# The mixers' row scales: column sums by a ones matrix, or one-column products and transposes

## The chip, the cores and the metric

The kernel runs on one core of one Trainium2 chip. The metric is the device time of one execution in microseconds (us). The engines are named as the profile names them: PE is TensorE (its matmuls), PEld its loads of the stationary operand, DVE is VectorE, ACT is ScalarE, POOL is GpSimd, and SP is SyncE, whose queue issues the loads of the weights.

## What is computed

A decoder trunk of two layers over 256 tokens and 1024 channels in float32. Each layer is a half-step FFN, a mixer and a second half-step FFN:

```python
for l in range(DEPTH):
    x = x + 0.5 * swiglu_ffn(x, ffn1_norm[l], ffn1_wi[l], ffn1_wo[l])
    h = rms_norm(x, mix_norm[l])
    (sb_q, sb_k, sb_v, mla_cq, ..., merge_gate) = jnp.split(h @ w_in[l], offsets, axis=-1)
    o_sb, o_mla, o_nsa = ...                  # three attentions on parts of h @ w_in
    y = sum of sigmoid(gate_i) * (o_i @ proj_i)
    x = x + y @ w_out[l]
    x = x + 0.5 * swiglu_ffn(x, ffn2_norm[l], ffn2_wi[l], ffn2_wo[l])
```

What matters here is the norm at the head of the mixer. `rms_norm(x, g)` divides each token's row by the root of its mean square over the 1024 channels and multiplies by the gain `g`. The division is by one number per token, so the kernel leaves it out of the projection and applies it to the projection's results.

## The kernel before

`x` is kept transposed: channels on the 128 partitions, in eight blocks, with the 256 tokens (two tiles of 128) along the row. Products are taken in `fp32r` from a high and a low half of each operand (`mm3` and its like: high by high, high by low, low by high). ACT makes the high half by a copy, DVE the low half by a subtraction. Weights come from HBM as parts of 128 by at most 512 (`raw`, six buffers, issued by SP) and are split by ACT (`whi`, line 998 in a mixer) and DVE (`wlo`, line 1000).

**How the squares come about.** At the end of an FFN, `out_T` adds the output to `x` (line 675), makes the halves `hThi` and `hTlo` of `x` times the gain for what follows (lines 599 and 600), and gathers the squares in the tile `sq`: ACT squares (line 608), DVE adds (lines 610 and 612), so that `sq[:, 0:256]` holds for each token 128 partial sums, one on each partition.

**The scales.** `scales` (line 1063) makes of it what the mixer needs, once per mixer. It splits `sq` into two halves (`split`, lines 573 and 574), and `col_sums` (line 614) multiplies a matrix of ones by both halves, which puts every token's sum of squares on all 128 partitions (tile `att`). `row_scales` (line 623) picks the diagonal with the identity (line 626), reduces it to a sum per token with tokens on the partitions (line 628), scales it (line 630), takes the power -1/2 on POOL (line 632), and makes three multiples of the result, `rn` (line 635). It then puts `rn` on the diagonal again (line 636) and splits that into the same two halves. A second `col_sums` spreads it over all partitions with the tokens along the row (tile `tp`), and ACT copies it to `rows` (tile `rowm`, line 1084). `rn` scales results that have tokens on the partitions, `rows` those that have them along the row.

**What sets the order.** In a mixer the order of PE, ACT and DVE is laid down while the kernel is built, by a small planner (`Planner`): each piece of work is a generator that asks, by `yield`, for an engine with a length, a latency, the events it depends on, and buffers. The planner grants the request that can start first by its own clock, adjusted by a hold for each generator (`HOLDS`), and the generator then issues its instructions. Each engine runs them in that order. The instructions that a generator issues behind one request stand together, also those on another engine than the one it asked for. `scales` comes first among the generators. Its first request is only for a `wr` buffer, and the split of `sq` follows at once; `col_sums` comes at the request of line 1070, all of `row_scales` at that of line 1073, and the second `col_sums` at that of line 1080 (`use_t(2, ...)`), with a request for POOL (line 1076) and two for DVE (lines 1077 and 1079) between, behind which nothing is issued.

**What runs around it.** `bulk` issues the projections: `lat` (line 1119) with 440 columns in `mm3` (lines 578 to 580), which uses the first four slabs of weights, two of them converted already in the FFN, and then `chunk_T` with 256 columns (lines 1159 to 1161). `weights` issues the loads and conversions of the slabs. `ev_lat` (line 1088) takes up the results of `lat` with `rn`, `sb_qk` (line 1167) those of `chunk_T` with `rows`.

The FFNs have a chain of their own with the same helpers (`spread_rn`, `scale_cols`).

Of the kernel before, what the change touches and what calls it, by code (L numbers as in the profile page):

```python
# [10 lines left out]
F = mybir.dt.float32  # L11
R = mybir.dt.float32r
AF = mybir.ActivationFunctionType
OP = mybir.AluOpType
AX = mybir.AxisListType

D = 1024
S = 256
DEPTH = 2
DFF = 2816  # L20
EPS = 1e-6
NT = 2
# [285 lines left out]
def use_v(n, *deps, slots=()):  # L308

    return "V", 0.065 + 0.00106 * n, 0.15 + 0.00106 * n, deps, slots  # L310
# [7 lines left out]
def use_a(n, *deps, slots=()):  # L318

    return "A", 0.085 + 0.00085 * n, 0.19 + 0.00085 * n, deps, slots  # L320
# [13 lines left out]
def use_t(count, *deps, slots=()):  # L334

    o = 0.2 + count * 0.109
    return "P", o, o + 0.2, deps, slots


def use_g(us, *deps, slots=()):  # L340

    return "G", us, us, deps, slots
# [13 lines left out]
MOVING = 48  # L356
# [5 lines left out]
NG = 3 * DEPTH * KT  # L362
# [9 lines left out]
def decoder_trunk(ctx, tc, xt_in, wts, lcon, cst, out, depth=DEPTH):  # L372
    nc = tc.nc
# [4 lines left out]
    sm = ctx.enter_context(tc.tile_pool(name="sm", bufs=5))  # L378
# [9 lines left out]
    def tp_tile():  # L388
        return pb.tile([128, 512], F, tag="ps", name="tp")

    def att_tile():
        return pb.tile([128, 512], F, tag="ps", name="att")
# [15 lines left out]
    ident = cp.tile([128, 128], F, name="ident")  # L408
# [33 lines left out]
    mh = cp.tile([128, 16], F, name="mh")  # L442
    nc.vector.memset(mh, -0.5)
    gcol = cp.tile([128, 128], F, name="gcol")
    ones = cp.tile([128, 128], R, name="ones")
    nc.vector.memset(ones.bitcast(F), 1.0)

# [124 lines left out]
    def split(hi, lo, src):  # L572
        nc.scalar.activation(hi, src, AF.Copy)
        nc.vector.tensor_sub(lo, src, hi)
# [39 lines left out]
    def col_sums(q, o):  # L614

        for i in range(2):
            nc.tensor.matmul(o, ones, q[i], start=i == 0, stop=i == 1)

    def ident2():

        return ident[:, None, :].to_broadcast([128, NT, 128])

    def row_scales(a, sq, parts):

        d = sq[:, 0:S].rearrange("p (t n) -> p t n", t=NT)
        nc.vector.tensor_tensor(d, a[:, 0:S].rearrange("p (t n) -> p t n", t=NT), ident2(), op=OP.mult)
        cs = sm.tile([128, 16], F, tag="mn", name="cs")
        nc.vector.tensor_reduce(cs[:, 0:NT], d, axis=AX.X, op=OP.add)
        ss = sm.tile([128, 16], F, tag="ss", name="ss")
        nc.vector.tensor_scalar(ss[:, 0:NT], cs[:, 0:NT], 1.0 / D, EPS, op0=OP.mult, op1=OP.add)  # L630
        r = sm.tile([128, 16], F, tag="rs", name="rs")
        nc.gpsimd.tensor_tensor(r[:, 0:NT], ss[:, 0:NT], mh[:, 0:NT], op=OP.pow)
        q = hp.tile([128, 8], F, tag="rn", name="rn", bufs=4)
        for i, m in enumerate((1.0, 0.5, 0.125)):
            nc.vector.tensor_scalar(q[:, 2 * i:2 * i + 2], r[:, 0:2], m, None, op0=OP.mult)
        nc.vector.tensor_tensor(d, ident2(), q[:, 0:2, None].to_broadcast([128, NT, 128]), op=OP.mult)
        split(*parts, sq[:, 0:S])
        return [q[:, 0:6].rearrange("p (m t) -> p m t", t=NT)[:, :, t] for t in range(NT)]

    nxt = [None]  # L640
# [63 lines left out]
    def ffn(l, gi):  # L704
# [5 lines left out]
        with ExitStack() as es:  # L710
# [71 lines left out]
            def scale_cols():  # L782
                a = att_tile()
                col_sums(sqr, a[:, 0:S])
                rn[:] = row_scales(a, sq, sqr)
# [118 lines left out]
    def mixer(l):  # L904
        es = ExitStack()
        mp = es.enter_context(tc.tile_pool(name="mp", bufs=1))
        hT, sq = nxt[0]
        nxt_T = hT
        hT = of_t(hT)
        rn = [None] * NT  # L910
        xd = dp.tile([NT, 128, D], F, tag="xd", name="xd")

        def wf():
            return mp.tile([128, 384], F, tag="wf", name="wf", bufs=4)

        def wr():
            return mp.tile([128, 2, 384], R, tag="wr", name="wr", bufs=WR_BUFS)
# [34 lines left out]
        s_wf, s_wr, s_qk, s_th, s_tmp, s_of = Slots(4), Slots(WR_BUFS), Slots(4), Slots(TH_BUFS), Slots(1), Slots(1)  # L952
# [109 lines left out]

        def scales():

            yield "-", 0.0, 0.0, (), (s_wr,)
            w = wr()
            sqr = [w[:, i, MOVING:MOVING + S] for i in range(2)]
            split(*sqr, sq[:, 0:S])
            k = yield "P", 0.4, 0.6, (Tok(10.5), ev_used[3]), (s_tp,)
            a = att_tile()  # L1070
            col_sums(sqr, a[:, 0:S])
            k = yield "V", 0.1, 0.17, (k,), ()
            rn[:] = row_scales(a, sq, sqr)
            s_tp.put(k)
            k = yield use_g(1.5, k)
            k = yield "V", 0.3, 0.4, (k,), ()
            ev_rn.set(k)
            k = yield use_v(256, k)
            k = yield use_t(2, k, slots=(s_tp,))
            tp = tp_tile()  # L1080
            col_sums(sqr, tp[:, 0:S])
            s_wr.put(k)
            k = yield use_a(256, k)
            nc.scalar.activation(rows, tp[:, 0:S], AF.Copy)
            s_tp.put(k)
            ev_rows.set(k)
# [931 lines left out]
        for th, hold in zip((scales(), tables(), sb_T(), sb_scores(), sb_pv(), cmp_in(), nsa_prep(), gates(), mla_T(),  # L2018
                             mla_scores(), mla_P(), mla_pv(), nsa_T(), k_chain(), v_chain(), cmp_scores(), nsa_scores(),
                             nsa_P(), nsa_pv(), bulk()), HOLDS):  # L2020
            spawn(th, hold)
# [57 lines left out]
```

## Time and profile before

| | |
|---|---|
| median of three timed runs | 1270.21 us (1269.59 to 1271.56) |
| the profiled execution, its own time | 1272.12 us |
| its span, from the first to the last instruction | 1270.2 us |
| PE busy | 1252.7 us, 99% |
| DVE, ACT busy | 940.2 us (74%), 787.8 us (62%) |
| HBM read, written | 254.91 MB, 34.60 MB |

A line of the timeline has the start in us from the beginning of the span, the length in us, the engine, the line of the kernel, the operation, what it writes and reads, the shape, and the number of like instructions that follow one another (their length is then that of the whole row); in brackets stands for how long the engine had been idle and what ended that. A matmul's start on PE follows its load on PEld, and neighbours overlap, so that 256 columns last 0.28 us each but follow one another at 0.11 us.

### The profile page before, as it was taken

The page shows a single profiled execution, that of the slowest core. Times are in us where ns is not written, and L with a number is a line of the kernel's source. Part 1 is how long each engine was busy: PE and PEld are TensorE (multiplying, and loading weights), DVE is VectorE, ACT ScalarE, POOL GpSimd, SP SyncE. Part 2 cuts the span into 40 slices and gives each one's busy share as a digit, 9 for nine tenths or more (in the row PEclk, how much of TensorE's full clock was granted, in tenths as well). Part 3 has the DMA queues.
Part 4 walks back from the last instruction along what each step waited for, and adds up shares of the span by engine and source line. Part 5 has one row for each costly group of instructions (what it writes and reads, how often), then busy time and mean ns, then how long its engine had stood idle before and what let it go on. Part 6 is the DMA issues. An engine that isn't in the chain of part 4 may idle for free.

```text
span 1270.2 us, 26119 instructions
## 1 busy us (share of the span) xinstructions
PE 1252.7 (99%) x9373; PEld 1167.5 (92%) x9373; DVE 940.2 (74%) x1963; ACT 787.8 (62%) x1632; POOL 105.5 (8%) x164
## 2 busy tenths in 40 slices
PE   9999998999999999999999999999999999999998
PEld 9999998888877899999999999988888779999987
DVE  7866677988898777676678676779868886776643
ACT  6555555687877566555556565567757774565542
POOL 0011110210000001122000121011100000000000
PEclk9999999999999999999999999999999999999999
DMA  8779985647545568899857899565786455666753
GB/s 285 261 273 331 323 298 175 199 151 238 188 125 172 173 206 257 278 325 334 282 201 267 290 327 346 190 206 168 251 289 216 142 174 181 186 186 194 217 163 119
DMA packets 150961, 291.76 MB, mean 230 GB/s; under 512 B 17840, under 2 KB 19504, under 8 KB 150832
## 3 DMA queue, kind: packets, MB, share of 16 engines
q1 hardware_dynamic: 140976, 258.12, 63.0%
q0 software_dynamic: 9856, 31.99, 6.5%
q8 instruction: 73, 1.20, 0.4%
q14 instruction: 56, 0.46, 0.1%
HBM read 254.91 MB, written 34.60 MB: 228 GB/s over the span
## 4 chain that ended last, share of the span: by engine, by line
PE 89%; DVE 4%; ACT 4%; DMA 2%; issue 1%; POOL 0%; ACTq 0%; DVEq 0%; POOLq 0%
PE acc L747 12%; PE acc L746 12%; PE acc L745 12%; PE acc L578 8%; PE acc L580 8%; PE acc L579 8%; PE acc L658 6%; PE acc L656 6%; PE acc L657 6%; DMA raw<-in_wts 1%; PE tp L1605 1%; PE acc L1159 1%; PE acc L1160 1%; PE acc L1161 1%; ACT wf L1564 1%
## 5 line engine op out<-in xcount | busy, mean ns | idle before, releaser
L745 PE MATMUL acc<-hThi,vhi 128*128 128x256 f32 x1280 | 354.1, 277 | 0.0
L746 PE MATMUL acc<-hTlo,vhi 128*128 128x256 f32 x1280 | 353.5, 276 | 0.0
L747 PE MATMUL acc<-hThi,vlo 128*128 128x256 f32 x1280 | 353.5, 276 | 0.0
L526 DVE TENSOR_TENSOR vlo<-raw,vhi 128x512 fp32r<-128x512 f32 x452 | 292.1, 684 | 74.7 <-ACT vhi L525 71.4
L525 ACT ACTIVATE vhi<-raw 128x512 fp32r<-128x512 f32 x452 | 263.0, 622 | 123.9 <-DMA raw<-in_wts 35.8
L745 PEld LDWEIGHTS acc<-hThi,vhi 128*128 128x128 f32 x1280 | 240.4, 188 | 0.0
L746 PEld LDWEIGHTS acc<-hTlo,vhi 128*128 128x128 f32 x1280 | 240.3, 188 | 0.0
L747 PEld LDWEIGHTS acc<-hThi,vlo 128*128 128x128 f32 x1280 | 240.2, 188 | 0.0
L1000 DVE TENSOR_TENSOR wlo<-raw,whi 128x512 fp32r<-128x512 f32 x216 | 140.3, 678 | 27.5 <-ACT whi L998 26.2
L998 ACT ACTIVATE whi<-raw 128x512 fp32r<-128x512 f32 x216 | 124.9, 616 | 44.0 <-issue 16.5
L658 PE MATMUL acc<-gh,vlo 128*128 128x256 f32 x528 | 146.4, 277 | 0.4 <-DVE vlo L526 0.3
L656 PE MATMUL acc<-gh,vhi 128*128 128x256 f32 x528 | 146.3, 277 | 0.0
L657 PE MATMUL acc<-gl,vhi 128*128 128x256 f32 x528 | 146.2, 277 | 0.0
L578 PE MATMUL acc<-whi,hThi 128*128 128x512 f32 (+2 forms) x352 | 137.7, 391 | 3.1 <-ACT whi L998 3.1
L579 PE MATMUL acc<-wlo,hThi 128*128 128x512 f32 (+2 forms) x352 | 133.6, 380 | 0.5 <-DVE wlo L1000 0.5
L580 PE MATMUL acc<-whi,hTlo 128*128 128x512 f32 (+2 forms) x352 | 133.6, 379 | 0.0
L545 DVE TENSOR_TENSOR elo<-eraw,ehi 128x512 fp32r<-128x512 f32 x60 | 41.4, 689 | 97.6 <-ACT ehi L544 97.6
L544 ACT ACTIVATE ehi<-eraw 128x512 fp32r<-128x512 f32 x60 | 37.9, 631 | 117.5 <-DMA eraw<-in_wts 116.1
L526 DVE TENSOR_TENSOR wlo<-raw,whi 128x512 fp32r<-128x512 f32 x108 | 69.9, 682 | 43.2 <-ACT whi L525 42.6
L658 PEld LDWEIGHTS acc<-gh,vlo 128*128 128x128 f32 x528 | 99.1, 188 | 0.8 <-DVE vlo L526 0.8
L657 PEld LDWEIGHTS acc<-gl,vhi 128*128 128x128 f32 x528 | 99.5, 188 | 0.0
L656 PEld LDWEIGHTS acc<-gh,vhi 128*128 128x128 f32 x528 | 99.1, 188 | 0.2 <-ACT vhi L525 0.2
(342 smaller groups left out, 2483.5 us busy)
## 6 DMA issues: line engine op xcount, KB each, us to landing
raw<-in_wts SPq DMA_DIRECT2D x764, 256.0 KB, 3.5
eraw<-in_wts SPq DMA_DIRECT2D x60, 256.0 KB, 5.3
early<-ehi POOLq DMA_DIRECT2D x60, 256.0 KB, 3.7
early<-elo POOLq DMA_DIRECT2D x60, 256.0 KB, 4.3
whi<-early SPq DMA_DIRECT2D x60, 256.0 KB, 3.9
wlo<-early SPq DMA_DIRECT2D x60, 256.0 KB, 4.0
xd<-x SPq DMA_DIRECT2D x4, 512.0 KB, 2.6
x<-xd SPq DMA_DIRECT2D x4, 512.0 KB, 3.7
```

The costliest lines, as they stand in the source:

```text
L525: nc.scalar.activation(hi[:, c:c + m], raw[:, :m], AF.Copy)
L526: nc.vector.tensor_tensor(lo[:, c:c + m], raw[:, :m], hi[:, c:c + m], op=OP.subtract)
L578: nc.tensor.matmul(o, a[0], b[0], start=start, stop=False)
L579: nc.tensor.matmul(o, a[0], b[1], start=False, stop=False)
L580: nc.tensor.matmul(o, a[1], b[0], start=False, stop=stop)
L656: nc.tensor.matmul(o, sl[0][:, w], h, start=k == 0 and c == 0, stop=False)
L657: nc.tensor.matmul(o, sl[0][:, w], l_, start=False, stop=False)
L658: nc.tensor.matmul(o, sl[1][:, w], h, start=False, stop=k == kts - 1 and c == 1)
L745: nc.tensor.matmul(o, sl[0][:, w], h, start=k == 0 and c == 0, stop=False)
L746: nc.tensor.matmul(o, sl[0][:, w], l_, start=False, stop=False)
L747: nc.tensor.matmul(o, sl[1][:, w], h, start=False, stop=k == KT - 1 and c == 1)
L1000: nc.vector.tensor_tensor(hl[1][:, c:c + m], raw[:, :m], hl[0][:, c:c + m], op=OP.subtract)
```

## The change

The mixers' `scales` no longer splits `sq`. The sums of squares come from two products, one for each tile of 128 tokens, with the tile of `sq` in float32 as the stationary operand and one column of ones (16 columns of ones are written to `gcol` at the kernel's start) as the moving one: the sums arrive with the tokens on the partitions, in a column each. `row_scales` in this form has no diagonal to pick and none to make. For `rows`, DVE copies each tile's `rn` column over 128 columns of a `wf` buffer, and PE transposes the two tiles. The requests to the planner keep engine, length and latency; the `wr` buffer is no longer asked for and a `wf` buffer is. The FFNs call `row_scales` as before.

```diff
     gcol = cp.tile([128, 128], F, name="gcol")
+    nc.vector.memset(gcol[:, NG:NG + 16], 1.0)
...
-    def row_scales(a, sq, parts):
-
-        d = sq[:, 0:S].rearrange("p (t n) -> p t n", t=NT)
-        nc.vector.tensor_tensor(d, a[:, 0:S].rearrange("p (t n) -> p t n", t=NT), ident2(), op=OP.mult)
-        cs = sm.tile([128, 16], F, tag="mn", name="cs")
-        nc.vector.tensor_reduce(cs[:, 0:NT], d, axis=AX.X, op=OP.add)
+    def row_scales(a, sq=None, parts=None):
+
+        if sq is not None:
+            d = sq[:, 0:S].rearrange("p (t n) -> p t n", t=NT)
+            nc.vector.tensor_tensor(d, a[:, 0:S].rearrange("p (t n) -> p t n", t=NT), ident2(), op=OP.mult)
+            a = sm.tile([128, 16], F, tag="mn", name="cs")
+            nc.vector.tensor_reduce(a[:, 0:NT], d, axis=AX.X, op=OP.add)
         ss = sm.tile([128, 16], F, tag="ss", name="ss")
-        nc.vector.tensor_scalar(ss[:, 0:NT], cs[:, 0:NT], 1.0 / D, EPS, op0=OP.mult, op1=OP.add)
+        nc.vector.tensor_scalar(ss[:, 0:NT], a[:, 0:NT], 1.0 / D, EPS, op0=OP.mult, op1=OP.add)
...
-        nc.vector.tensor_tensor(d, ident2(), q[:, 0:2, None].to_broadcast([128, NT, 128]), op=OP.mult)
-        split(*parts, sq[:, 0:S])
+        if sq is not None:
+            nc.vector.tensor_tensor(d, ident2(), q[:, 0:2, None].to_broadcast([128, NT, 128]), op=OP.mult)
+            split(*parts, sq[:, 0:S])
...
         def scales():
 
-            yield "-", 0.0, 0.0, (), (s_wr,)
-            w = wr()
-            sqr = [w[:, i, MOVING:MOVING + S] for i in range(2)]
-            split(*sqr, sq[:, 0:S])
             k = yield "P", 0.4, 0.6, (Tok(10.5), ev_used[3]), (s_tp,)
             a = att_tile()
-            col_sums(sqr, a[:, 0:S])
+            for t in range(NT):
+                nc.tensor.matmul(a[:, t:t + 1], sq[:, t * 128:(t + 1) * 128], gcol[:, NG:NG + 1], start=True, stop=True)
             k = yield "V", 0.1, 0.17, (k,), ()
-            rn[:] = row_scales(a, sq, sqr)
+            rn[:] = row_scales(a)
             s_tp.put(k)
             k = yield use_g(1.5, k)
             k = yield "V", 0.3, 0.4, (k,), ()
             ev_rn.set(k)
-            k = yield use_v(256, k)
+            k = yield use_v(256, k, slots=(s_wf,))
+            b = wf()
+            for t in range(NT):
+                nc.vector.tensor_copy(b[:, t * 128:(t + 1) * 128], rn[t][:, 0:1].to_broadcast([128, 128]))
             k = yield use_t(2, k, slots=(s_tp,))
             tp = tp_tile()
-            col_sums(sqr, tp[:, 0:S])
-            s_wr.put(k)
+            for t in range(NT):
+                nc.tensor.transpose(tp[:, t * 128:(t + 1) * 128], b[:, t * 128:(t + 1) * 128], ident)
+            s_wf.put(k)
```

## The prediction

> **What bounds the kernel now.** The page comes first: it says which engine fills the span.
>
> ```profile
> span 1270.2 us, 26119 instructions
> ## 1 busy us (share of the span) xinstructions
> PE 1252.7 (99%) x9373; PEld 1167.5 (92%) x9373; DVE 940.2 (74%) x1963; ACT 787.8 (62%) x1632; POOL 105.5 (8%) x164
> ```
>
> PE is at work for 1252.7 of 1270.2 us, so all its idle time is 17.5 us. An edit beside PE gains nothing unless PE waits for it, and an instruction added on PE costs its own time. So the second view is the list of PE's waits (in total, times, longest).
>
> ```profile
> PE tp L617 <- ACT wr L573: 4.1, 2, 2.6
> PE acc L578 <- ACT whi L998: 3.1, 2, 1.6
> PE acc L579 <- DVE wlo L1000: 0.5, 2, 0.3
> ```
>
> These are the three places of the mixer's front where PE waits, each twice, once per layer, 7.7 of the 17.5 us. The first is the spread of the scales (L617, `col_sums` into `tp`), behind a split on ACT. The other two are the start of the mixer: the third weight slab's first half is converted late. The third view, the timeline engine by engine, shows why. The start in layer 0 on ACT, on DVE, on PE:
>
> ```profile
> 193.10 0.61 ACT L608 ACTIVATE sq<-x 128x512 f32<-128x512 f32 x1
> 194.98 0.42 ACT L573 ACTIVATE wr<-sq 128x256 fp32r<-128x256 f32 x1 [1.27 <-PE acc L580]
> 195.30 1.94 ACT L998 ACTIVATE whi<-raw 128x512 fp32r<-128x512 f32 x4
> ```
>
> ```profile
> 194.47 0.42 DVE L612 TENSOR_TENSOR sq<-sq 128x256 f32<-128x256 f32 x1
> 195.43 0.43 DVE L574 TENSOR_TENSOR wr<-sq,wr 128x256 fp32r<-128x256 f32 x1 [0.53 <-ACT wr L573]
> 195.95 1.14 DVE L1000 TENSOR_TENSOR wlo<-raw,whi 128x512 fp32r<-128x512 f32 x2
> ```
>
> ```profile
> 195.97 0.47 PE L578 MATMUL acc<-whi,hThi 128*128 128x440 f32 x1 [1.51 <-ACT whi L998]
> 196.69 0.47 PE L579 MATMUL acc<-wlo,hThi 128*128 128x440 f32 x1 [0.26 <-DVE wlo L1000]
> ```
>
> ACT finishes its last square at 193.71 and has weights to convert (four conversions run without a gap once they begin, so their data had landed). But the first instruction of `scales`, the split of `sq` (L573), stands ahead of them, and it needs the finished sum of squares, which DVE ends at 194.89 (194.47 + 0.42). DVE then loses its turn too: it waits 0.53 for ACT's half, subtracts (L574), and only then makes the first `wlo`. PE needs that `wlo` at L579.
>
> The spread, in layer 1, on DVE, on ACT, on PE:
>
> ```profile
> 832.46 1.94 DVE L1000 TENSOR_TENSOR wlo<-raw,whi 128x512 fp32r<-128x512 f32 x3 [2.91 <-ACT whi L998]
> 834.32 0.42 DVE L626 TENSOR_TENSOR sq<-att,ident 128x256 f32<-128x256 f32 x1
> 834.77 0.42 DVE L628 TENSOR_REDUCE cs<-sq 128x2 f32<-128x256 f32 x1
> 835.22 0.17 DVE L630 TENSOR_SCALAR ss<-cs 128x2 f32<-128x2 f32 x1
> 836.29 0.31 DVE L635 TENSOR_SCALAR rn<-rs 128x2 f32<-128x2 f32 x3 [0.89 <-POOL rs L632]
> 836.50 0.42 DVE L636 TENSOR_TENSOR sq<-ident,rn 128x256 f32<-128x256 f32 x1
> 837.46 0.43 DVE L574 TENSOR_TENSOR wr<-sq,wr 128x256 fp32r<-128x256 f32 x1 [0.54 <-ACT wr L573]
> 837.81 1.28 DVE L1000 TENSOR_TENSOR wlo<-raw,whi 128x512 fp32r<-128x512 f32 x2
> ```
>
> ```profile
> 831.80 2.41 ACT L998 ACTIVATE whi<-raw 128x512 fp32r<-128x512 f32 x4 [2.97 <-DMA raw<-in_wts]
> 837.02 0.42 ACT L573 ACTIVATE wr<-sq 128x256 fp32r<-128x256 f32 x1 [2.80 <-DVE sq L636]
> ```
>
> ```profile
> 834.59 0.28 PE L1161 MATMUL acc<-hThi,wlo 128*128 128x256 f32 x1
> 837.49 0.84 PE L617 MATMUL tp<-wr,ones 128*128 128x256 f32 x2 [2.62 <-ACT wr L573]
> 838.17 0.28 PE L1159 MATMUL acc<-hThi,whi 128*128 128x256 f32 x1
> ```
>
> PE stands in its fixed order before L617 while DVE and ACT pass the scales back and forth: mask, reduce, POOL's power, mask again, ACT's half, DVE's half. From the mask (834.32) to PE's next projection product (838.17) is 3.85 us. Layer 0 has the same chain, from 205.03 to 208.90, 3.87:
>
> ```profile
> 205.03 0.42 DVE L626 TENSOR_TENSOR sq<-att,ident 128x256 f32<-128x256 f32 x1
> ```
>
> ```profile
> 206.34 0.28 PE L1161 MATMUL acc<-hThi,wlo 128*128 128x256 f32 x1
> 208.13 0.97 PE L617 MATMUL tp<-wr,ones 128*128 128x256 f32 x2 [1.51 <-ACT wr L573]
> 208.90 0.41 PE L1159 MATMUL acc<-hThi,whi 128*128 128x256 f32 x1
> ```
>
> There the projection products afterwards last 0.41 instead of 0.28. The table of windows gives the cause (columns: length, then busy time of PE, PEld, DVE, ACT, POOL, then PEclk, DMA share, GB/s):
>
> ```profile
> 208.90:212.10 3.20, 3.20 (x16) 3.20 (x16) 2.58 (x9) 2.90 (x13) 1.34 (x2) 0.50 0.48 152
> ```
>
> PE ran at half its clock for 3.20 us behind a wait of 1.51, which cost about 1.6 us of work. Layer 1, with the longer wait of 2.62, shows no such stretch.
>
> **The change, part by part.** The planner's order first: each request of `scales` keeps its engine, length and latency, and only the buffers asked for differ (`wr` goes, one `wf` of four comes, well ahead of any shortage). So I take every other instruction to keep its place. What is issued at those places changes.
>
> *Start.* L573 and L574 go. ACT can convert from 193.71 and DVE can make the first `wlo` right behind L612, at 194.89 instead of 195.95: 1.06 us earlier. By then ACT's first `whi` is done (193.71 + 0.62 is 194.33), so DVE ends last, and PE's L579 moves with it from 196.69 to about 195.63. The two layers' waits are alike (3.1 in two, the longest 1.6), so 2 x 1.06 = 2.12 us. No DMA is moved; the loads that follow wait for a raw buffer that the first L1000 frees, so they go 1.06 earlier as well.
>
> *Sum of squares.* Two products over 256 columns go, and two over one column, with `sq` itself in f32 as the stationary operand, come. Rows for both sides:
>
> ```profile
> 202.69 0.31 PEld L617 LDWEIGHTS att<-wr,ones 128*128 128x128 f32 x2
> ```
>
> ```profile
> 313.96 0.36 PEld L1605 LDWEIGHTS tp<-ident,wf 128*128 128x128 f32 x3
> ```
>
> The old pair holds PE for 0.24 (two loads 0.12 apart). The trace has no f32 product, only f32 transposes: three loads of a 128x128 f32 tile in 0.36, so 0.11 apart. At that rate the new pair is 0.22, nothing lost. The other end is the longest step of PE quoted above, 0.47 a product: 0.94, a loss of 0.70. I take a loss of 0.30 per mixer, 0.6 in all, nearer to the transposes, whose operand has the same shape and type. All of it is on PE's path. The Trainium skill's page "FP8 and Floating Point Precision", section "TensorE Precision Notes", has true fp32 take four passes; at 0.11 a pass, an estimate, that is 0.88 for the pair, a loss of 1.28 over both mixers and a forecast 0.7 later; no run here shows it yet.
>
> *Spread.* Off the chain: the mask, the reduction, the second mask, both splits. On it: the scaling of the sums, POOL's power, three small scalings, then what DVE has queued before the copies, two copies of a 128x128 tile, two transposes. In layer 1 the scaling begins at 834.32 in place of L626. From it to the first small scaling is 1.07 (835.22 to 836.29), and 0.21 more to the next instruction (836.50): 835.60. The two copies are not issued with `row_scales` but two requests later, and in the planner's order one `wlo` lies between, the first of the two now at 837.81 (1.28 for two of 0.68, so 0.60 each): 836.20. For a copy the nearest row is
>
> ```profile
> L1300 DVE COPY mk<-krb x4: 279/287/295, 253.1 to 884.5; 128x256 f32<-128x256 f32 x4
> ```
>
> with 0.29 for twice the columns; I take 0.28 each as the upper end and half as the lower. That gives 836.76. From DVE's last half to PE's next projection is now 0.28 (837.46 + 0.43 to 838.17), so PE goes on at 837.04: 1.13 earlier. With layer 0's equal chain, 2 x 1.15 = 2.3 us, and 2.8 with copies of half that length. The `wlo` between is covered today: its `whi` is one of the four that ACT ends at 834.21, 1.39 ahead of its turn. ACT no longer waits 2.80 for L636, so the conversion behind L573 moves ahead as well; nobody waits for that.
>
> *At the kernel's start* DVE fills 16 columns of `gcol`:
>
> ```profile
> 1.41 0.17 DVE L446 MEMSET ones<- 128x128 f32 x1
> 4.30 0.48 DVE L600 SCALAR_TENSOR_TENSOR hTlo<-xt,hThi 128x256 fp32r<-128x256 f32 x1 [2.73 <-ACT hThi L599]
> ```
>
> This is shorter than the 0.17 beside it, in 2.73 us of idle DVE: nothing; without that cover, under 0.17.
>
> *Sum.* 2.12 + 2.3 - 0.6 = 3.8 us, plus the half clock. After the change PE waits about 0.8 at the start and 0.6 before the transposes, so I expect the 1.6 us stretch of layer 0 to be gone. Against the profiled execution's own time, 1272.12 (span 1270.2 and 1.9 around it), that makes 1272.12 - 3.8 - 1.6 = 1266.7. The median of the timed runs, 1270.21, lies 1.9 below that execution, so the runs at the median may not have had the stretch; I credit half of it: 1270.21 - 3.8 - 0.8 = **1265.6 us**.
>
> **The rivals.** *The landings hold their time.* ACT's four conversions of layer 1 wait 2.97 for raw weights, and DVE's L626 stands behind their `wlo`. Should these loads land when they do now, though asked for 1.06 earlier, the sums would begin no earlier, and PE would stand longer before the transposes by what it gained at the start. The same price would come if something other than L573 holds ACT at the start: its row of layer 0 names PE's L580 as the last to release it. Against both: each load waits for a buffer that moves, and L573 began 0.09 after DVE's L612 ended. Time: 1270.21 - 2.3 + 0.6 - 0.8 = 1267.7. Chance 0.14.
>
> *The half clock stays and comes twice.* If even short waits trip it in both mixers, the credit of 0.8 goes and 1.6 comes: 1268.0. For it: 1.51 of waiting preceded a stretch; against it: 2.62 did not. Chance 0.08. The Trainium skill's "TensorE: Matmul & The Clock Gate", section "What's actually happening", halves the clock only after an idle window of about 3.4 us, which would put this rival out; the trace disagrees, with 1.51.
>
> *The weight part becomes the wait: slower.* The `wlo` that now runs after the spread will run between POOL's power and the copies, so PE comes to depend on its raw load. From 1.39 us of delay on, each further microsecond costs one per mixer. About 5 us late in both layers gives 1265.6 + 2 x 3.6 = 1272.8. For it: DMA already holds ACT for 2.97 there; against it: four parts come in one burst. Chance 0.05.
>
> *It does nothing:* the waits move to the next PE instructions that need scaled accumulators; 1270.2. Chance 0.05, as nothing on PE in the lists waits on those.
>
> **How the numbers follow.** The forecast keeps 0.68. Its best end is copies of half length, no loss on the products and the whole stretch: 1270.21 - 2.12 - 2.8 - 1.6 = 1263.7. Its own worst end is a loss of 1.4 on the products and no stretch: 1270.21 - 2.12 - 2.3 + 1.4 = 1267.2. The range goes on past the first two rivals to 1268.8, where 1 in 10 or so is left above. A difference under 0.2% (2.54 us, so 1267.67 to 1272.75) can't be told from none here. Faster takes 0.65 of the forecast, nearly half of the first rival and a little of the second: 0.74; same 0.21; slower 0.05.
>
> **What would show it.** Right: no L573 ahead of the mixer's first L998, PE's L579 about 1.1 us sooner after L612, PE's wait before the transposes under 1 us, two one-column products of 0.1 to 0.5 each, no half-clock stretch in either mixer. Wrong: a product near 1 us, copies behind two `wlo` instead of one, L998 still late at the start (then another wait than L573 held ACT), or raw landings at their old distance from the start of the mixer.

## The result and the profile after

The changed kernel takes 1263.13 us (median of six runs, 1261.11 to 1265.52), the kernel before 1270.94 in the same comparison: a ratio of 0.9936, 95% interval 0.992 to 0.9952. The forecast was 1265.6 with a range from 1263.7: the direction was right, the gain larger than the range allowed. The profiled execution took 1263.93, its span is 8.4 us shorter than before. Its page:

```profile
span 1261.8 us, 26118 instructions
## 1 busy us (share of the span) xinstructions
PE 1250.0 (99%) x9377; PEld 1165.8 (92%) x9377; DVE 935.5 (74%) x1958; ACT 786.7 (62%) x1628; POOL 105.5 (8%) x164
```

PE's idle time fell from 17.5 to 11.8 us. The list of PE's waits (in total, times, longest; the changed file has its lines 1 to 4 further down, so L998 is now L1001, L1000 is L1003, L578 to L580 are L579 to L581):

```profile
PE acc L421 <- DVE warm L418: 1.5, 1, 1.5
PE tp L1729 <- DMA zc<-wf: 1.2, 1, 1.2
PE tp L1609 <- ACT wf L1600: 0.9, 2, 0.6
PE acc L748 <- DVE gate L764: 0.8, 1, 0.8
PE acc L659 <- ACT vhi L526: 0.6, 1, 0.6
PE acc L579 <- DVE hvl L1029: 0.5, 1, 0.5
PE acc L579 <- ACT hThi L600: 0.5, 1, 0.5
PE acc L750 <- DVE vlo L527: 0.5, 1, 0.5
PE acc L661 <- DVE vlo L527: 0.4, 1, 0.4
PE acc L581 <- DVE hTlo L601: 0.3, 1, 0.3
```

All three rows of before are gone, and not only shortened. No PE wait on `wlo` or on the first conversion is left at the mixers' starts, and none before the transposes (L1085) either. The prediction had expected 0.8 and 0.6 us to stay there. New at layer 0's start are a wait of 0.5 for `hThi` (L600) and one of 0.3 for `hTlo` (L601). The timeline of ACT at layer 0's start shows what the prediction missed:

```profile
185.81 0.63 ACT L1001 ACTIVATE whi<-raw 128x512 fp32r<-128x512 f32 x1 [0.90 <-DMA raw<-in_wts]
186.77 0.51 ACT L1001 ACTIVATE whi<-raw 128x368 fp32r<-128x368 f32 x1 [0.33 <-DMA raw<-in_wts]
188.01 0.63 ACT L1001 ACTIVATE whi<-raw 128x512 fp32r<-128x512 f32 x1 [0.73 <-DMA raw<-in_wts]
188.96 0.51 ACT L1001 ACTIVATE whi<-raw 128x368 fp32r<-128x368 f32 x1 [0.32 <-DMA raw<-in_wts]
191.40 0.91 ACT L600 ACTIVATE hThi<-x,gcol 128x256 fp32r<-128x256 f32 x2 [1.93 <-DVE x L678]
```

```profile
196.27 0.62 ACT L609 ACTIVATE sq<-x 128x512 f32<-128x512 f32 x1
196.79 1.14 ACT L1001 ACTIVATE whi<-raw 128x512 fp32r<-128x512 f32 x2
198.04 0.91 ACT L600 ACTIVATE hThi<-x,gcol 128x256 fp32r<-128x256 f32 x2
198.86 0.62 ACT L609 ACTIVATE sq<-x 128x512 f32<-128x512 f32 x1
199.38 2.18 ACT L1001 ACTIVATE whi<-raw 128x512 fp32r<-128x512 f32 x4
```

Six of the mixer's conversions (L1001) now stand inside the FFN's tail: four ahead of the first `hThi` of the mixer, two ahead of the last. Before, all of them stood behind L573. DVE has their `wlo` (L1003) in the same places, and an instruction of the tail that was behind another may now be ahead of it. So the order of ACT and DVE at the seam is not the planner's alone. The code places by hand only PE's order for the whole kernel; ACT and DVE are placed by hand within a mixer, and the kernel's builder merges that list with the FFN's instructions. In the kernel before, the list begins with the split of `sq`, which needs the end of the FFN's chain, and everything behind it had to wait. In the changed kernel the list begins with conversions whose data come early.

The move has a price as well. DVE comes to the tail's next instruction (L764) only behind four of these `wlo`; what follows it on the way to `hThi` is late, and so is PE's first product of the mixer:

```profile
188.68 1.37 DVE L1003 TENSOR_TENSOR wlo<-raw,whi 128x512 fp32r<-128x512 f32 x2 [0.82 <-ACT whi L1001]
189.96 0.68 DVE L764 TENSOR_TENSOR u<-acc,rows 128x512 f32<-128x512 f32 x1
191.96 0.47 PE L579 MATMUL acc<-whi,hThi 128*128 128x440 f32 x1 [0.47 <-ACT hThi L600]
```

In a second profile of the changed kernel (`e7_after_again` below) this wait is absent, and in `e3_sums_only` it is 1.3.

DVE and PE, later in the same mixer:

```profile
204.48 0.15 DVE L632 TENSOR_SCALAR ss<-att 128x2 f32<-128x2 f32 x1
205.46 0.31 DVE L637 TENSOR_SCALAR rn<-rs 128x2 f32<-128x2 f32 x3 [0.83 <-POOL rs L634]
205.68 0.69 DVE L1003 TENSOR_TENSOR wlo<-raw,whi 128x512 fp32r<-128x512 f32 x1
206.28 0.35 DVE L1081 COPY wf<-rn 128x128 f32<-128x128 f32 x2
```

```profile
207.53 0.28 PE L1165 MATMUL acc<-hThi,wlo 128*128 128x256 f32 x1
207.65 0.38 PE L1085 MATMUL tp<-ident,wf 128*128 128x128 f32 x2
207.78 0.36 PE L1163 MATMUL acc<-hThi,whi 128*128 128x256 f32 x1
```

The copies end at 206.63, and PE comes to the transposes at 207.65, a full microsecond later: nothing waits. The row of L1003 between L637 and L1081 is the weight part that the prediction had placed there.

PE's products stand in the same order in both kernels, apart from those of `scales`, so one can subtract their starts:

| stretch | after minus before, us |
|---|---|
| first FFN, up to its last product | +1.8 |
| first two slabs of layer 0's mixer (behind the wait for `hThi`) | +0.9 |
| its third and fourth slab (2.3 of waits gone, 0.6 lost at `hTlo`) | -1.7 |
| its sums and spread | -2.1 |
| to layer 1's mixer (the half-clock stretch is gone, 1.4, and the wait for `zc` 0.3 shorter) | -1.7 |
| start of layer 1's mixer | -2.4 |
| its sums and spread | -3.1 |
| the rest | -0.2 |

Together -8.5. The 1.8 lost in the first FFN are not the change's: in `e7_after_again` the same stretch is 2.1 us shorter than before's. The 0.9 behind the wait for `hThi` are.

### The profile page after: what moved, and what is told of

Read it like the earlier page. It is cut to its first block, busy times and chain, and to the rows that moved or that the text cites. A ratio compares the mean times of both kernels' runs of the same rounds, so it can differ in the third digit from the quotient of the medians.

```text
span 1261.8 us, 26118 instructions
## 1 busy us (share of the span) xinstructions
PE 1250.0 (99%) x9377; PEld 1165.8 (92%) x9377; DVE 935.5 (74%) x1958; ACT 786.7 (62%) x1628; POOL 105.5 (8%) x164
## 4 chain that ended last, share of the span: by engine, by line
PE 82%; DMA 6%; DVE 5%; ACT 4%; issue 2%; SPq 0%; POOL 0%; ACTq 0%; DVEq 0%; POOLq 0%
PE acc L748 11%; PE acc L749 11%; PE acc L750 11%; PE acc L579 9%; PE acc L581 8%; PE acc L580 8%; PE acc L659 4%; PE acc L660 4%; PE acc L661 4%; DMA eraw<-in_wts 3%; DMA raw<-in_wts 2%; DVE vlo L527 1%; PE acc L1163 1%; PE acc L1165 1%; PE tp L1609 1%
## 5 line engine op out<-in xcount | busy, mean ns | idle before, releaser
L1003 DVE TENSOR_TENSOR wlo<-raw,whi 128x512 fp32r<-128x512 f32 x216 | 140.8, 678 | 25.7 <-ACT whi L1001 24.3
L1001 ACT ACTIVATE whi<-raw 128x512 fp32r<-128x512 f32 x216 | 125.2, 616 | 48.4 <-PE acc L581 16.9
L579 PE MATMUL acc<-whi,hThi 128*128 128x512 f32 (+2 forms) x352 | 137.7, 391 | 0.5 <-ACT hThi L600 0.5
L581 PE MATMUL acc<-whi,hTlo 128*128 128x512 f32 (+2 forms) x352 | 133.7, 380 | 0.3 <-DVE hTlo L601 0.3
L580 PE MATMUL acc<-wlo,hThi 128*128 128x512 f32 (+2 forms) x352 | 133.3, 379 | 0.0
```

Source lines behind the costliest of these rows:

```text
L579: nc.tensor.matmul(o, a[0], b[0], start=start, stop=False)
L580: nc.tensor.matmul(o, a[0], b[1], start=False, stop=False)
L581: nc.tensor.matmul(o, a[1], b[0], start=False, stop=stop)
L1003: nc.vector.tensor_tensor(hl[1][:, c:c + m], raw[:, :m], hl[0][:, c:c + m], op=OP.subtract)
```

## The experiments

Theory A: the excess over the forecast is the six conversions that moved into the FFN's tail. Theory B: the place of everything is as predicted, and the costs in the sum (copies, products, clock) were sized too high. In the first four experiments PE's products keep the order that they have in the kernel before, apart from those of `scales`.

**The order held fast.** The changed kernel, with two tiny instructions at the head of the mixer's list that wait for the end of the FFN's squares:

```diff
         def scales():
 
+            pin = sm.tile([128, 16], F, tag="mn", name="pin")
+            yield "-", 0.0, 0.0, (), ()
+            nc.scalar.activation(pin[:, 0:1], sq[:, 512:513], AF.Copy)
+            nc.vector.tensor_scalar(pin[:, 1:2], sq[:, 0:1], 1.0, None, op0=OP.mult)
             k = yield "P", 0.4, 0.6, (Tok(10.5), ev_used[3]), (s_tp,)
```

> The changed kernel, with two tiny instructions put first in the mixer's order: ACT copies one column of the last squares (its own L609), DVE one column of the finished sq, both into a tile that nobody reads. So no weight conversion of the mixer can stand ahead of the end of the FFN: this is the order that the prediction assumed. Theory A (the excess over the prediction is six conversions that moved ahead into the FFN's tail): the time is about what was predicted, 1265.6, that is 5 us below the kernel before and 2 to 3 above the changed kernel; PE waits about 0.8 us for a wlo at each mixer's start. Theory B (place unchanged, but copies, products and the clock were sized too high): as fast as the changed kernel, 1263.1, with no wait of PE over 0.3 at the mixers' start.

Measured: 1266.18 us, 0.9962 of the kernel before (0.9946 to 0.9978). The forecast of 1265.6 is 0.9964 of 1270.21, so the whole comes out as forecast. Against the changed kernel's 0.9936 it gives back 0.0026, 3.3 us. Those two intervals touch, but `e3_sums_only` below, run beside this kernel with the order left free, took 1262.54, 3.6 us less (1261.32 to 1265.01, against 1263.69 to 1268.08 here). The waits come back where the prediction had put them; on DVE and PE at layer 1's start:

```profile
820.52 0.42 DVE L613 TENSOR_TENSOR sq<-sq 128x256 f32<-128x256 f32 x1
820.98 0.15 DVE L1071 TENSOR_SCALAR pin<-sq 128x1 f32<-128x1 f32 x1
821.06 3.40 DVE L1003 TENSOR_TENSOR wlo<-raw,whi 128x512 fp32r<-128x512 f32 x6
```

```profile
820.58 0.47 PE L579 MATMUL acc<-whi,hThi 128*128 128x440 f32 x1 [0.17 <-ACT whi L1001]
821.81 0.47 PE L580 MATMUL acc<-wlo,hThi 128*128 128x440 f32 x1 [0.76 <-DVE wlo L1003]
```

Two instructions over one column, which take 0.20 on ACT and 0.15 on DVE, thus cost some 3 us over the two mixers by where they stand. This is theory A; B expected no loss. The spread of layer 1 in the same run:

```profile
830.08 0.15 DVE L632 TENSOR_SCALAR ss<-att 128x2 f32<-128x2 f32 x1
831.13 0.31 DVE L637 TENSOR_SCALAR rn<-rs 128x2 f32<-128x2 f32 x3 [0.90 <-POOL rs L634]
831.35 0.69 DVE L1003 TENSOR_TENSOR wlo<-raw,whi 128x512 fp32r<-128x512 f32 x1
831.95 0.35 DVE L1085 COPY wf<-rn 128x128 f32<-128x128 f32 x2
```

```profile
831.66 0.28 PE L1169 MATMUL acc<-hThi,wlo 128*128 128x256 f32 x1
832.27 0.42 PE L1089 MATMUL tp<-ident,wf 128*128 128x128 f32 x2 [0.33 <-PE acc L1169]
832.44 0.36 PE L1167 MATMUL acc<-hThi,whi 128*128 128x256 f32 x1
```

From the scaling (830.08) to PE's next projection product (832.44) is 2.36 us; the prediction had worked out 2.72, and before it was 3.85. The two copies take 0.35 together, not 0.56, and the product starts 0.14 after their end (832.30), not 0.28.

**Only the place.** The kernel before, with the split of `sq` later in the planner's order and nothing else changed:

```diff
-            yield "-", 0.0, 0.0, (), (s_wr,)
+            yield "-", 0.0, 0.0, (Tok(7.0),), (s_wr,)
             w = wr()
```

> The kernel before, with its arithmetic and instructions all kept; only the first request of scales, behind which the split of sq is issued, depends on a planner time of 7.0, so that it comes after the first six conversions in the mixer's order. Theory A: PE's waits at the two mixers' starts go (2.2 each, about 4 in all), and the long chain of the spread begins earlier, so that 0.5 to 1 us of wait per mixer stays before L617: 1264 to 1266. Theory B: placing alone gives nothing more than the 1.06 per mixer of the prediction's start: 1268 to 1269.

Measured: 1265.41, 0.9959 (0.9945 to 0.9973). By the medians more than half of the change's gain (0.0041 of 0.0064) comes with none of its arithmetic. The list of PE's waits has no row of the start's conversions any more, and its first row is what the long chain of the spread leaves:

```profile
PE tp L617 <- ACT wr L573: 2.1, 2, 1.1
```

A had expected 0.5 to 1 us per mixer there, and it is 1.0 and 1.1. B's 1268 to 1269 lies outside the interval.

**One half, the sums.** One-column products, but the spread as before (the edit is to the changed kernel; `rnq` holds the row of scales of `row_scales`):

```diff
             rn[:] = row_scales(a)
+            w = wr()
+            sqr = [w[:, i, MOVING:MOVING + S] for i in range(2)]
+            d = sq[:, 0:S].rearrange("p (t n) -> p t n", t=NT)
+            nc.vector.tensor_tensor(d, ident2(), rnq[0][:, 0:2, None].to_broadcast([128, NT, 128]), op=OP.mult)
+            split(*sqr, sq[:, 0:S])
...
-                nc.vector.tensor_copy(b[:, t * 128:(t + 1) * 128], rn[t][:, 0:1].to_broadcast([128, 128]))
...
-                nc.tensor.transpose(tp[:, t * 128:(t + 1) * 128], b[:, t * 128:(t + 1) * 128], ident)
...
+            col_sums(sqr, tp[:, 0:S])
```

> Half of the change: sums of squares by one-column products as in the changed kernel, but the spread by the diagonal, its two halves and ones as before. Theory A: the six conversions move ahead as in the changed kernel; the chain from the scaling to the products of the spread is about 3.0 us instead of 2.2, and the changed kernel had 1 us to spare there: 1263 to 1264, equal to the changed kernel. Theory B: only the start's 2.1 and the shorter chain of 0.9 per mixer: 1267.

Measured: 1262.54, 0.994 (0.9927 to 0.9953): not told apart from the whole change. So copies and transposes bring nothing here that shows. What counts is that nothing at the head of the list waits for `sq`. That the mask and the reduction ahead of POOL are gone as well fits the 0.0019 between `e2_late_split` and this run: the wait of 2.1 before L617 that stays there is absent from this run's list of waits. The two intervals overlap, so this second part is read from the waits and not shown by the times.

**The other half, the spread.** Sums as before, with their split at the head of the list; copies and transposes for the spread. With `None`, `row_scales` leaves out the second diagonal and the second split:

```diff
-            rn[:] = row_scales(a, sq, sqr)
+            rn[:] = row_scales(a, sq, None)
...
+            b = wf()
+            for t in range(NT):
+                nc.vector.tensor_copy(b[:, t * 128:(t + 1) * 128], rn[t][:, 0:1].to_broadcast([128, 128]))
...
-            col_sums(sqr, tp[:, 0:S])
...
+            for t in range(NT):
+                nc.tensor.transpose(tp[:, t * 128:(t + 1) * 128], b[:, t * 128:(t + 1) * 128], ident)
```

> The other half: sums of squares by the split, ones and the diagonal as before, first in the mixer's order, but the spread by copies and transposes. Theory A: the start keeps its waits of 1.5 and 0.3 per mixer; the spread's chain gets 1.1 to 1.3 shorter in each mixer, and the half-clock stretch may go: 1267 to 1268.5. Theory B: the shorter spread carries most of the gain: 1265 or less.

Measured: 1267.14, 0.9981 (0.997 to 0.9993). The waits at the start are all there, and the one before the spread is shorter:

```profile
PE acc L578 <- ACT whi L999: 3.3, 2, 1.7
PE tp L1087 <- DVE wf L1083: 2.6, 2, 1.3
```

So the spread's edit is worth 0.0019 (0.0007 to 0.003) behind a split at the head, and nothing that shows once the conversions are early. Theory A had 1267 to 1268.5, B 1265 or less.

**What is left.** The longest wait that remains in the middle of the changed kernel is PE's for `zc`, a DMA whose landing the planner reckons at 3.0 us after ACT's copy. Two kernels change that number alone, to 5.0 (`e5_zc5`) and to 6.5 (`e6_zc6`):

```diff
-            z = Tok(k2.t + 3.0)
+            z = Tok(k2.t + 5.0)
```

> The changed kernel with one planner number changed: the landing of the compressed keys' rearrangement (zc, a DMA through POOL's queue) is reckoned at 5.0 instead of 3.0 after ACT's copy, so that PE's transposes of zc are placed later. The longest wait left in the changed kernel's middle is PE for this DMA: 1.2 there, 1.9 to 2.4 in the experiments. If the wait is what it costs, 1 to 2 us less than the changed kernel (1261 to 1262 where that has 1263); if the planner's new order makes another wait of the same size, no difference.

> The same with 6.5 instead of 5.0. If the wait for zc had been over 1.5 in most executions, a little faster than with 5.0; if the order as a whole decides, no more than 1 us from the changed kernel in either direction.

Measured: 1265.98, 0.9964 (0.9951 to 0.9976), and 1261.02, 0.9926 (0.9913 to 0.9938). With 5.0 the wait for `zc` falls to 0.4, and the new order brings waits of up to 1.0 in other places of the mixer. The ratio is 0.0028 above that of the changed kernel's first comparison, a loss that neither branch of the expectation had. With 6.5 the wait goes and little comes for it. Both orders of PE differ from the changed kernel's in the middle of the mixer, so an effect of the order as a whole is likely; it was not taken apart. To see whether 6.5 beats the change, both ran once more side by side:

> The changed kernel itself, once more, on the same chip as the next run: 0.994 of the kernel before, as at first.

> The changed kernel with the landing of zc reckoned at 6.5: if its first result was more than the scatter, 1 to 2 us below the changed kernel of the same call, with intervals that hardly overlap; if not, the same.

Measured: the changed kernel 1262.53, 0.9936 (0.9911 to 0.9961), and 6.5 in the planner 1261.87, 0.9921 (0.99 to 0.9943). The intervals lie over each other, so it is not shown to be faster. The changed kernel's ratio is the same as in its first comparison.

## Why the prediction was wrong

The direction, the three waits as the place of the gain, and the chain behind them were right. The step that failed is "So I take every other instruction to keep its place". Six conversions of each mixer moved ahead into the FFN's tail instead, and holding them back (`e1_pinned`) costs some 3.3 us, where the forecast missed by 2.5. Inside the sum, the term of the spread was sized too small as well, 1.15 where 2.1 and 2.8 were measured even with the order held fast.

*Start.* Forecast 1.06 us per mixer. Measured 1.7 and 2.4, since ACT and DVE had made the first parts before the tail ended; in layer 0, 0.6 of 2.3 was lost again, as the last `hTlo` comes later behind the conversions, and another 0.9 at the first `hThi`. In `e7_after_again`, which has neither of these two waits, the start gains 2.3 and 2.4. Where the assumed order was enforced (`e1_pinned`), PE's third slab came 0.7 and 0.9 earlier, close to the forecast. The reason given for the term, the split ahead of the conversions, holds (`e2_late_split`); how far they would then move was not asked.

*Sum of squares.* The forecast was a loss of 0.30 per mixer. The timeline of PE:

```profile
203.67 0.28 PE L1165 MATMUL acc<-hThi,wlo 128*128 128x256 f32 x1
203.79 0.50 PE L1071 MATMUL att<-gcol,sq 128*128 128x1 f32 x4
204.15 0.36 PE L1163 MATMUL acc<-hThi,whi 128*128 128x256 f32 x1
204.35 0.28 PE L1164 MATMUL acc<-hTlo,whi 128*128 128x256 f32 x1
```

From the first one-column product (203.79) to the second projection product behind the pair (204.35) is 0.56; less the 0.12 of one projection product that is 0.44 for the pair, 0.20 more than the 0.24 of before. The size was about right, and 0.88, the estimate from the Trainium skill's page "FP8 and Floating Point Precision" (section "TensorE Precision Notes"), was twice the measured time.

*Spread.* Forecast 1.15 per mixer; measured 2.3 and 3.3, and 2.1 and 2.8 with the order held fast. Of this the shorter chain is 1.5 (3.85 to 2.36 with the order held fast, where 1.13 was forecast, as the copies were taken at 0.56 instead of 0.35 and the step behind them at 0.28 instead of 0.14). The rest is that the chain starts earlier against PE: the scaling begins 7.3 and 6.7 us after PE's first `wlo` product of the third slab (8.0 and 8.3 in `e1_pinned`), where the mask of before began 8.3 and 9.4 after it. In all three kernels DVE comes to it straight from a `wlo`, and these weight parts come earlier: ahead of them ACT waited 1.90 and 2.97 for raw weights before, 0.47 and 0.71 in `e1_pinned`, and for none in the changed kernel. Why the loads land that much earlier in `e1_pinned` too stays open. In the changed kernel the chain ends before PE arrives, and shortening it further gains nothing that shows (`e3_sums_only`).

That the time of `e1_pinned` meets the forecast is thus in part luck. By the two profiles its starts, sums and spreads gain 6.1 us (0.7 and 0.9, -0.4, 2.1 and 2.8), and its span of 1264.3 is 5.9 below before's; only the medians are 3.8 apart, the size of the forecast's sum. The profiled execution of before was 1.9 above its median.

*The half clock.* Half of 1.6 us was credited. The changed kernel's first profile has no such stretch in its span; its second, like `e1_pinned` and `e3_sums_only`, has one behind the wait for `zc`. So the change removed the wait ahead of layer 0's stretch, but not every stretch. The record has the mean granted clock of the timed runs. Of 43 runs of the kernel before beside the experiments, 5 had 1.000, with a median of 1269.92; of 12 of the changed kernel, 6 had it, with 1262.46. With the clock out of it the two are still 7.5 us apart, where the sum without the credit was 3.8. These are few runs, on several chips, but the clock can't be what was missing.

*The rivals.* None of them was it: the landings did not hold their time but came earlier, the weight part between POOL's power and the copies was never late, and no half-clock stretch came in the front of either mixer in the two profiles of the changed kernel. The range had to be open towards an order of ACT and DVE at the seam that is better than assumed, and it was not, for all its cases kept that order.

## What to carry to other kernels

Where a list of instructions that is ordered by hand is merged with others by the builder, its first instruction decides how early all the rest can go: look at what it waits for, and ask for an edit that removes it what will move ahead of it, not only what stands right behind it. Two instructions of 0.2 us or less at the head of each mixer's list cost some 3 us in all by their place. And before a long chain is made shorter, see by how much it is late once the other edits are in: here the same edit was worth 2.4 us, or nothing that shows.

## What the hardware showed that was not expected

A product of f32 operands over one column shows as two loads and two matmuls (four rows of L1071 for two products), 0.12 us apart, 0.22 a product.

The stretches of 3.41 us at half the clock came behind PE waits of 1.51 (layer 0's spread before), 2.18, 1.9 and 2.27 (for `zc`, in `e1_pinned`, `e3_sums_only` and the second profile of the changed kernel), and not behind waits of 2.62 (layer 1's spread before), 2.1 and 2.4 (for `zc`, in `e2_late_split` and `e4_spread_only`). The window of `e1_pinned`:

```profile
279.71:283.13 3.42, 3.42 (x9) 2.67 (x8) 3.25 (x6) 2.22 (x6) 0.00 (x0) 0.50 0.42 108
```

What decides between them stays open. The length of the wait alone does not, and PE's busy time in the 3.41 us ahead does not either: 1.82 in 205.28 to 208.69 of the kernel before, which a stretch followed, against 1.54 in 833.33 to 836.74 of the same profile, which none did.
